# A decoder trunk on one core: the roots of the last row tiles' norms on GpSimd, and sums that keep their place in the program

## The chip, the core and the metric

The kernel runs on one core of a Trainium2 chip. Its time is the device time of one execution in microseconds, the median of several runs. The engines are TensorE (PE; PEld is its weight load), VectorE (DVE), ScalarE (ACT), GpSimd (POOL) and SyncE (SP), which issues the transfers here. Each engine works through its own queue in order, and semaphores tie the queues together.

## What is computed

One layer of a hybrid decoder for a prompt of 2048 rows and a group of 32 sample rows. The change lies in its end: the mixed groups (2048 columns, `mix`) go through the output projection, are normalised, added to the residual, and normalised again:

```python
def rms_norm(x, g):
    xf = x.astype(jnp.float32)
    y = xf * lax.rsqrt(jnp.mean(xf * xf, axis=-1, keepdims=True) + EPS)
    return (y * g.astype(jnp.float32)).astype(x.dtype)
...
    out = rms_norm(mix @ w_out, post_g)
    return x + out, conv_new, pool_new, k, v
...
    y_prompt = rms_norm(xp, final_g)
```

So each row of the output needs two reciprocal roots: one of the mean square of the projection's row, one of the mean square of the row after the residual is added.

## The kernel before

The earlier stages (norm and input projection, sample group, causal attention of the prompt, convolution) are not touched. In the last stage the 2048 rows are 16 row tiles of 128, taken as 8 pairs i = 0 to 7; i = 8 (`LAST`) stands for the sample rows, which are row tile 16 in the closings. The product `mix @ w_out` is done by a scheme of seven products of half sized blocks, numbered 1 to 7, in which sums and differences of blocks save the eighth. A part is (product, pair, half of its depth): 12 matmuls, each factor split into a high and a low piece (`mh`, `ml` for the rows, `wohi`, `wolo` for the weights), and three products of pieces for each of 4 slices: high by high, high weights' low piece, and last the rows' low piece. TensorE takes the parts in the order of the list `order`: products 1, 7, 2, 6, then 4, 5 and 3, pair by pair. For pairs 3 to 7 that is (4,i), (5,i), (3,i), two halves each.

For each part, in the order of the program: `out_load` (SP brings the rows, L1648 on), `out_combine` (L1694: a sum or difference of two blocks, on GpSimd at L1699, L1702 and L1706, on VectorE at L1705), `out_high` (ScalarE casts to the high piece, L1714), `out_low` (VectorE subtracts to get the low piece, L1725), and the matmuls (L1969). For product 5 the combination is the sum of the two blocks that product 4 loaded, in the tile `mr4_i_h`, at L1699. A part is combined four parts ahead of the one that TensorE is given.

When a product is done, `out_ready` (L1731) joins it with the others. For products 4, 5 and 3 VectorE adds the partial sums `U2` or `U3` (L1768, L1769), ScalarE squares the result and sums it by row (`square`, L1727), and VectorE multiplies it in place by the post factor `gpost` (L1772). Product 5 completes row tile 2i + 1, product 3 row tile 2i, and each is then closed by `out_tile` (L1790): a root of the first mean square (add L1798, root L1799, reciprocal L1800), two products with the residual's row `oxt` added (L1804), two squares (L1805), a second root (L1808 to L1810), a product with the final factor (L1815), and the transfer out (L1817). For even tiles the first half of the row comes back from DRAM as `oh`, with the factor put on by GpSimd (L1788). The two roots' values are columns of a small tile, `oss`, of which there is one buffer. For tile 14, the last, the work of tile 15's end is written between its steps, and its output goes in two halves.

The order on an engine is not that of the text: a scheduler moves instructions ahead where it takes their inputs to be there. `tc.keep_in_program_order` pins one behind the instruction that was written before it on the same engine.

Of the kernel before, what the change touches and what calls it, by code (L numbers as in the profile page):

```python
# [8 lines left out]
F32 = mybir.dt.float32  # L9
# [3 lines left out]
AF = mybir.ActivationFunctionType  # L13
ALU = mybir.AluOpType
# [4 lines left out]
P = 128  # L19
D = 1024  # L20
# [28 lines left out]
RAWS = 4  # L49
# [38 lines left out]
def kernel(  # L88
# [72 lines left out]
                       pattern=[[-1, P]], channel_multiplier=1)  # L161
    ones_ln = con.tile([P, P], F32, name="ones_ln")
    pool.memset(ones_ln, 1.0 / 512)
    eps_t = con.tile([P, 1], F32, name="eps_t")
    pool.memset(eps_t, EPS)
    first = zc.tile([P, 1], F32, name="first")

    table = [act.activation(out=first, in_=eps_t, func=AF.Sqrt)]
# [1525 lines left out]
    def out_combine(x):  # L1694
        prod, i, h = x
        store()
        ts = raws[x]
        if prod == 5 and i < LAST:
            pool.tensor_tensor(out=ts[1], in0=ts[0], in1=ts[1], op=ALU.add)  # L1699
            ts = ts[1:]  # L1700
        elif prod == 7:
            pool.tensor_tensor(out=ts[0], in0=ts[0], in1=ts[1], op=ALU.subtract)  # L1702
            stores.append(((0, i, h), msd[0, i, h], ts[0]))
        elif prod == 6:
            tc.keep_in_program_order(dve.tensor_tensor(out=ts[0], in0=ts[0], in1=ts[1], op=ALU.subtract))  # L1705
            pool.tensor_tensor(out=ts[2], in0=ts[2], in1=ts[0], op=ALU.subtract)  # L1706
            stores.append(((1, i, h), msd[1, i, h], ts[2]))
        raws[x] = ts[0]

# [16 lines left out]

    def square(c, t, half):  # L1727
        rows = P if t < 16 else NS
        act.activation(out=junk[:rows], in_=c[:rows], func=AF.Square, accum_out=ssk[:rows, t, half : half + 1])

    def out_ready(prod, i, o):  # L1731

        if i == LAST:
            if prod == 5:
                return
            both = (ope.tile([P, 512], F32, tag="oh", name="both3", bufs=OH) if prod == 3 else
                    op.tile([P, 512], F32, name=f"both{prod}", bufs=1))
            act.copy(both[:NS], o[NS : 2 * NS])
            dve.tensor_tensor(out=both[:NS], in0=both[:NS], in1=o[:NS], op=ALU.add)
            if prod == 1:  # L1740
                keep["s"] = both
# [12 lines left out]
        if prod == 1:  # L1754
            act.copy(U2[:, i], o)
        elif prod == 7:
            dve.tensor_tensor(out=U3[:, i], in0=o, in1=U2[:, i], op=ALU.add)
        elif prod == 6:
            dve.tensor_tensor(out=U3[:, i], in0=o, in1=U3[:, i], op=ALU.add)
            dve.tensor_tensor(out=U2[:, i], in0=o, in1=U2[:, i], op=ALU.add)  # L1760
        elif prod == 2:
            c = opw.tile([P, 512], F32, tag="c11", name=f"c11_{i}", bufs=1)
            dve.tensor_tensor(out=c, in0=o, in1=U2[:, i], op=ALU.add)
            square(c, t, 0)
            sp.dma_start(c11d[i], c)
        else:
            if prod == 5:
                dve.tensor_tensor(out=U2[:, i], in0=o, in1=U2[:, i], op=ALU.add)  # L1768
            dve.tensor_tensor(out=o, in0=o, in1=(U2 if prod == 3 else U3)[:, i], op=ALU.add)  # L1769
            half = 0 if prod == 4 else 1  # L1770
            square(o, t, half)
            dve.tensor_tensor(out=o, in0=o, in1=gpost[:, 512 * half : 512 * half + 512], op=ALU.mult)  # L1772
            keep[t, half] = o
            if prod != 4:
                out_tile(t, keep[t, 0], keep[t, 1])
            if (prod, i) == (3, 0):
                out_first(2)
            if prod == 5 and i != 2 or (prod, i) == (3, 1):
                out_factor(2 if prod == 3 else i)
# [10 lines left out]
    def out_tile(t, a, b):  # L1790

        rows = P if t < 16 else NS
        xt = ope.tile([P, D], F32, tag="oxt", name=f"oxt{t}", bufs=OX)[:rows]
        sp.dma_start(xt, xp[P * t : P * t + P, :] if t < 16 else xs)
        if t != 14:
            keep["ss"] = ope.tile([P, 6], F32, tag="oss", name=f"oss{t}", bufs=1)
        ss = keep["ss"][:rows, 3:] if t == 14 else keep["ss"][:rows]
        dve.tensor_tensor(out=ss[:, 0:1], in0=ssk[:rows, t, 0:1], in1=ssk[:rows, t, 1:2], op=ALU.add)  # L1798
        act.activation(out=ss[:, 0:1], in_=ss[:, 0:1], func=AF.Sqrt, bias=eps_t[:rows], scale=1.0 / D)  # L1799
        dve.reciprocal(out=ss[:, 0:1], in_=ss[:, 0:1])  # L1800
        last = t == 14
        halves = (slice(0, 512), slice(512, 1024))
        for n, (hs, src) in enumerate(zip(halves, (a[:rows], b[:rows]))):
            dve.scalar_tensor_tensor(out=xt[:, hs], in0=src, scalar=ss[:, 0:1], in1=xt[:, hs], op0=ALU.mult, op1=ALU.add)  # L1804
            act.activation(out=junk[:rows], in_=xt[:, hs], func=AF.Square, accum_out=ss[:, n + 1 : n + 2])  # L1805
        if last:
            keep.pop("end")()
        dve.tensor_tensor(out=ss[:, 1:2], in0=ss[:, 1:2], in1=ss[:, 2:3], op=ALU.add)  # L1808
        act.activation(out=ss[:, 1:2], in_=ss[:, 1:2], func=AF.Sqrt, bias=eps_t[:rows], scale=1.0 / D)  # L1809
        dve.reciprocal(out=ss[:, 1:2], in_=ss[:, 1:2])  # L1810
        dst = y_prompt[0, P * t : P * t + P, :] if t < 16 else y_sample.rearrange("b t d -> (b t) d")

        def end():
            for n, hs in enumerate(halves if last else (slice(0, 1024),)):
                dve.scalar_tensor_tensor(out=xt[:, hs], in0=xt[:, hs], scalar=ss[:, 1:2], in1=gfin[:rows, hs],  # L1815
                                         op0=ALU.mult, op1=ALU.mult)
                (wq if n else sp).dma_start(dst[:, hs], xt[:, hs])  # L1817

        if t == 15:
            keep["end"] = end  # L1820
        else:
            end()
# [261 lines left out]
    for n, x in enumerate(parts):  # L2084
        if n == last_:
# [4 lines left out]
            gfin = ope.tile([P, D], F32, name="gfin", bufs=1)  # L2090
            sp.dma_start(gpost, post_g[0].partition_broadcast(P))
            sp.dma_start(gfin, final_g.partition_broadcast(P))
        prod, i, h = x
        if prod == 4 and not h and i != 2:
            out_first(i)
# [53 lines left out]
```

## Time and profile before

| | |
|---|---|
| median of 3 runs | 2359.39 us (2356.07 to 2364.3) |
| the profiled execution's own time | 2357.87 us |
| its span, first to last instruction | 2356.2 us |
| mean granted TensorE clock | 0.992 |
| TensorE, VectorE, ScalarE, GpSimd busy | 2268.6, 1718.0, 1118.3, 1280.6 us |

In the profile a row of a group gives line, engine, operation, output and inputs by tile name, shapes and count, then busy time and mean duration in ns, then the idle time of the engine ahead of it and what ended that. A row of a timeline gives start, duration and the same names, with the idle time before it in brackets. Names come without their numbers there: `acc` is a product's sum, `mr` a part's rows, `oss` the roots' tile.

### The profile page before, as it was taken

The page shows a single profiled execution, that of the slowest core. Times are in us where ns is not written, and L with a number is a line of the kernel's source. Part 1 is how long each engine was busy: PE and PEld are TensorE (multiplying, and loading weights), DVE is VectorE, ACT ScalarE, POOL GpSimd, SP SyncE. Part 2 cuts the span into 40 slices and gives each one's busy share as a digit, 9 for nine tenths or more (in the row PEclk, how much of TensorE's full clock was granted, in tenths as well). Part 3 has the DMA queues.
Part 4 walks back from the last instruction along what each step waited for, and adds up shares of the span by engine and source line. Part 5 has one row for each costly group of instructions (what it writes and reads, how often), then busy time and mean ns, then how long its engine had stood idle before and what let it go on. Part 6 is the DMA issues. An engine that isn't in the chain of part 4 may idle for free. (4 is left out here: it accounts for less than half of the span.)

```text
span 2356.2 us, 42223 instructions
## 1 busy us (share of the span) xinstructions
PE 2268.6 (96%) x16024; PEld 1767.5 (75%) x16024; DVE 1718.0 (73%) x2428; ACT 1118.3 (47%) x1947; POOL 1280.6 (54%) x1322
## 2 busy tenths in 40 slices
PE   7999999999999999999999999899999999999897
PEld 7998888888888777777777777555555557878775
DVE  5342786969647664577787868888897966787897
ACT  5322343342442322234242324788989875454554
POOL 3554545555464656545546463688988854432330
PEclk9999999999999999999999999999999999999999
DMA  6689977878678899987877884756544207866674
GB/s 212 196 283 298 343 267 257 288 248 289 243 262 314 311 352 338 322 287 260 304 264 257 280 273 143 176 170 165 161 131 117 77 23 225 283 223 215 208 247 159
DMA packets 336870, 557.94 MB, mean 237 GB/s; under 512 B 27986, under 2 KB 212434, under 8 KB 320267
## 3 DMA queue, kind: packets, MB, share of 16 engines
q1 hardware_dynamic: 281290, 286.53, 39.4%
q0 software_dynamic: 55376, 268.72, 32.0%
q8 instruction: 126, 2.06, 0.4%
q14 instruction: 78, 0.63, 0.1%
HBM read 465.09 MB, written 90.68 MB: 236 GB/s over the span
## 5 line engine op out<-in xcount | busy, mean ns | idle before, releaser
L966 DVE STREAM_TRANSPOSE T<-kt 128x1024 f32<-128x1024 f32 x256 | 308.6, 1225 | 182.8 <-PE sSA L979 170.0
L933 POOL DMA_INDIRECT vt<-in_cache_v_dram,idv x256 | 252.8, 988 | 255.5 <-PE sO L1018 194.9
L618 DVE SCALAR_TENSOR_TENSOR cacc<-U,par,cacc 128x512 f32<-128x512 f32 x480 | 359.7, 749 | 11.0
L1344 POOL TENSOR_TENSOR be<-be,E 128x512 f32<-128x512 f32 (+3 forms) x316 | 300.6, 967 | 60.4 <-DVE E L1335 26.6
L1335 DVE TENSOR_TENSOR_SCAN E<-gam,cr,ZM 128x513 f32<-128x513 f32 x192 | 232.7, 1262 | 14.1 <-ACT gam L1266 10.7
L933 POOL DMA_INDIRECT kt<-in_cache_k_dram,idk x128 | 128.3, 1002 | 198.8 <-DVE T L966 157.4
L1355 PEld LDWEIGHTS AT<-ident,be 128*128 128x128 f32 x1082 | 116.1, 141 | 128.0 <-ACT at L1361 48.2
L1969 PE MATMUL acc<-wohi,mh 128*128 128x512 f32 (+1 forms) x480 | 193.5, 403 | 1.9 <-ACT mh L1714 1.9
L1266 ACT ACTIVATE gam<-S,nbias_bc 128x1024 f32<-128x1024 f32 (+1 forms) x158 | 173.1, 1095 | 42.6 <-ACT be L1267 18.5
L1969 PE MATMUL acc<-wolo,mh 128*128 128x512 f32 (+1 forms) x480 | 189.5, 395 | 2.6 <-DVE wolo L1626 2.6
L1969 PE MATMUL acc<-wohi,ml 128*128 128x512 f32 x448 | 177.4, 396 | 5.6 <-DVE ml L1725 5.6
L1262 PE MATMUL S<-kT,Q 128*128 128x512 f32 (+1 forms) x632 | 174.6, 399 | 5.4 <-ACT be L1267 5.4
L1267 ACT ACTIVATE be<-S,bias_bc 128x1024 f32<-128x1024 f32 (+1 forms) x158 | 172.0, 1089 | 1.4 <-DMA gsd<-sg1sg 1.4
L1355 PE MATMUL AT<-ident,be 128*128 128x128 f32 x1082 | 157.3, 283 | 14.0 <-DVE at L1359 7.4
L1371 PE MATMUL av<-at,V 128*64 128x512 f32 (+3 forms) x640 | 152.2, 554 | 3.5 <-DVE sbo L1376 3.5
L979 PE MATMUL sSA<-T,W 128*32 128x128 f32 x4096 | 138.3, 276 | 1.8 <-DVE T L966 1.4
L979 PEld LDWEIGHTS sSA<-T,W 128*32 128x32 f32 x4096 | 104.6, 109 | 36.6 <-issue 29.1
L1018 PE MATMUL sO<-vt,saT 128*32 128x512 f32 x1024 | 122.3, 592 | 0.0
L1725 DVE TENSOR_TENSOR ml<-mr,mh 128x512 fp32r<-128x512 f32 x108 | 95.7, 897 | 35.0 <-ACT mh L1714 33.5
L1262 PEld LDWEIGHTS S<-kT,Q 128*128 128x128 f32 x632 | 105.0, 193 | 19.2 <-ACT be L1267 6.8
L1361 ACT COPY at<-AT 128x512 f32<-128x512 f32 x192 | 111.3, 679 | 12.2 <-PE AT L1355 12.2
L1332 DVE TENSOR_TENSOR_SCAN E<-gam,ZM 128x384 f32<-128x384 f32 (+1 forms) x124 | 94.3, 809 | 28.8 <-ACT gam L1266 22.0
(577 smaller groups left out, 6024.7 us busy)
## 6 DMA issues: line engine op xcount, KB each, us to landing
Q<-qd SPq DMA_DIRECT2D x64, 256.0 KB
mr<-mixd SPq DMA_DIRECT2D x32, 512.0 KB
mr<-mixd SPq DMA_DIRECT2D x48, 256.0 KB
xtp<-in_x_prompt_dram SPq DMA_DIRECT2D x16, 512.0 KB
kT<-kd SPq DMA_DIRECT2D x64, 128.0 KB
ws<-in_w_out_dram SPq DMA_DIRECT2D x16, 512.0 KB
wsd<-ws SPq DMA_DIRECT2D x16, 512.0 KB
msd<-mr SPq DMA_DIRECT2D x32, 256.0 KB
```

Of the source, the lines that this page charges most:

```text
L618: dve.scalar_tensor_tensor(out=ps, in0=U[:, a + k : a + k + H], scalar=wd[:, k : k + 1], in1=ps, op0=ALU.mult, op1=ALU.add)
L933: pool.indirect_dma_start(out=dst, out_offset=None, in_=rows, in_offset=bass.IndirectOffsetOnAxis(ap=idx, axis=0))
L966: S["turn"] = dve.transpose(T[:, 2 * hh : 2 * hh + 2].rearrange("p s j t -> p (s j t)"), kt[:, 2 * hh : 2 * hh + 2].rearrange("p s j d -> ...
L979: pe.matmul(sSs[n][32 * g : 32 * g + 32, P * ml : P * (ml + 1)], lhsT=W[:, jj, :], rhs=T[:, :, jj, :], start=i == 0, stop=i == 3, tile_pos ...
L1262: pe.matmul(S[:, j, :w], lhsT=Q[:, x, P * (q2 + j) : P * (q2 + j + 1)], rhs=kt[:, :w], start=x == 0, stop=x == 1)
L1266: act.activation(out=ga, in_=S[:, :, :w], func=AF.Sigmoid, bias=nbias_bc[:, h : h + 1], scale=-1.0)
L1267: act.activation(out=be, in_=S[:, :, :w], func=AF.Sigmoid, bias=bias_bc[:, h : h + 1])
L1335: dve.tensor_tensor_scan(out=E[:, j][:, ::-1], data0=g_[:, j][:, ::-1], data1=ZM[:, 0:1].to_broadcast([P, 513]), initial=carry[hh, q2][:, ...
L1344: newest.append(pool.tensor_tensor(out=be[:, j, :m], in0=be[:, j, :m], in1=E[:, j, 513 - w : 513 - w + m], op=ALU.mult).ins)
L1355: pe.transpose(ap_[:, P * qt : P * (qt + 1)], A[hp, qb, kc, hh, qt][:, P * r : P * (r + 1)], ident)
L1371: pe.matmul(av[64 * hh : 64 * hh + 64, c], lhsT=V[:, 4 * kc + r, 64 * hh : 64 * hh + 64], rhs=ats.pop((hp, qb, kc, r, hh))[:, c], start=dg ...
L1969: pe.matmul(o[:rows], lhsT=m[a][:, k, :rows], rhs=W[prod, 4 * h + k][w], start=not cont and h == k == n == 0, stop=h == 1 and k == 3 and n ...
```

## The change

Four things. The roots of row tiles 10 to 15 are two GpSimd instructions: one adds the two halves' mean squares and epsilon, one raises the sum to the power of -0.5. The other tiles keep their three instructions on VectorE and ScalarE. The mean's factor goes into the squares (`scale=D**-0.5`), so the roots need none. The post factor of products 4 and 5 is put on when product 5 is done, and for pair 7 into a tile of its own (`og`) instead of in place. GpSimd's sum of product 5 and its difference of product 6 are pinned. `oss` becomes one tile with two sets of four columns in turn.

```diff
-    eps_t = con.tile([P, 1], F32, name="eps_t")
+    two = con.tile([P, 2], F32, name="two")
+    eps_t, mhalf = two[:, 0:1], two[:, 1:2]
     pool.memset(eps_t, EPS)
+    pool.memset(mhalf, -0.5)
...
         if prod == 5 and i < LAST:
-            pool.tensor_tensor(out=ts[1], in0=ts[0], in1=ts[1], op=ALU.add)
+            tc.keep_in_program_order(pool.tensor_tensor(out=ts[1], in0=ts[0], in1=ts[1], op=ALU.add))
...
-            pool.tensor_tensor(out=ts[2], in0=ts[2], in1=ts[0], op=ALU.subtract)
+            tc.keep_in_program_order(pool.tensor_tensor(out=ts[2], in0=ts[2], in1=ts[0], op=ALU.subtract))
...
-        act.activation(out=junk[:rows], in_=c[:rows], func=AF.Square, accum_out=ssk[:rows, t, half : half + 1])
+        act.activation(out=junk[:rows], in_=c[:rows], func=AF.Square, scale=D**-0.5, accum_out=ssk[:rows, t, half : half + 1])
...
             square(o, t, half)
-            dve.tensor_tensor(out=o, in0=o, in1=gpost[:, 512 * half : 512 * half + 512], op=ALU.mult)
             keep[t, half] = o
             if prod != 4:
+                for n in (0, 1) if prod == 5 else (1,):
+                    c = keep[t, n]
+                    if i == LAST - 1:
+                        keep[t, n] = op.tile([P, 2, 512], F32, tag="raw", name=f"og{t}_{n}", bufs=RAWS)[:, 0]
+                    dve.tensor_tensor(out=keep[t, n], in0=c, in1=gpost[:, 512 * n : 512 * n + 512], op=ALU.mult)
                 out_tile(t, keep[t, 0], keep[t, 1])
...
-        dve.tensor_tensor(out=ss[:, 0:1], in0=ssk[:rows, t, 0:1], in1=ssk[:rows, t, 1:2], op=ALU.add)
-        act.activation(out=ss[:, 0:1], in_=ss[:, 0:1], func=AF.Sqrt, bias=eps_t[:rows], scale=1.0 / D)
-        dve.reciprocal(out=ss[:, 0:1], in_=ss[:, 0:1])
+        keep["turn"] = 4 - keep.get("turn", 4)
+        ss = oss[:rows, keep["turn"] : keep["turn"] + 4]
+
+        def root(k, a, b):
+            if not 10 <= t < 16:
+                dve.tensor_tensor(out=ss[:, k : k + 1], in0=a, in1=b, op=ALU.add)
+                act.activation(out=ss[:, k : k + 1], in_=ss[:, k : k + 1], func=AF.Sqrt, bias=eps_t[:rows])
+                dve.reciprocal(out=ss[:, k : k + 1], in_=ss[:, k : k + 1])
+                return
+            pool.tensor_scalar(out=ss[:, k : k + 1], in0=b, scalar1=a, scalar2=EPS, op0=ALU.add, op1=ALU.add)
+            pool.tensor_tensor(out=ss[:, k : k + 1], in0=ss[:, k : k + 1], in1=mhalf[:rows], op=ALU.pow)
+
+        root(0, ssk[:rows, t, 0:1], ssk[:rows, t, 1:2])
...
-        dve.tensor_tensor(out=ss[:, 1:2], in0=ss[:, 1:2], in1=ss[:, 2:3], op=ALU.add)
-        act.activation(out=ss[:, 1:2], in_=ss[:, 1:2], func=AF.Sqrt, bias=eps_t[:rows], scale=1.0 / D)
-        dve.reciprocal(out=ss[:, 1:2], in_=ss[:, 1:2])
+        root(3, ss[:, 1:2], ss[:, 2:3])
```

How this moves instructions is seen at three places. The first is GpSimd's queue from the sum for part (5,6,0) on, before the change. Here `mr4_6_1` and `mr4_7_1` are the sums for parts (5,6,1) and (5,7,1), and `oh2_i` the post factor on tile 2i's first half:

```order
L1699 TENSOR_TENSOR mr4_6_0_23612<-mr4_6_0_23612 128x512
L1699 TENSOR_TENSOR mr4_6_1_23633<-mr4_6_1_23633 128x512
L1788 TENSOR_TENSOR oh2_5_23596<-oh2_5_23596,gpost_22691 128x512
L1699 TENSOR_TENSOR mr4_7_0_23764<-mr4_7_0_23764 128x512
L1699 TENSOR_TENSOR mr4_7_1_23785<-mr4_7_1_23785 128x512
L1788 TENSOR_TENSOR oh2_6_23748<-oh2_6_23748,gpost_22691 128x512
L1788 TENSOR_TENSOR oh2_7_23902<-oh2_7_23902,gpost_22691 128x512
```

The same place after the change. The first "..." leaves out the six rows of the other three roots of tiles 11 and 10, the second the eight rows of tiles 13 and 12:

```order
L1701 TENSOR_TENSOR mr4_6_0_23603<-mr4_6_0_23603 128x512
L1794 TENSOR_TENSOR oh2_6_23733<-oh2_6_23733,gpost_22692 128x512
L1701 TENSOR_TENSOR mr4_7_0_23749<-mr4_7_0_23749 128x512
L1810 TENSOR_SCALAR oss_22696<-ssk_20133 128x1
L1811 TENSOR_TENSOR oss_22696<-oss_22696,two_93 128x1
...
L1701 TENSOR_TENSOR mr4_6_1_23623<-mr4_6_1_23623 128x512
L1794 TENSOR_TENSOR oh2_7_23881<-oh2_7_23881,gpost_22692 128x512
...
L1701 TENSOR_TENSOR mr4_7_1_23769<-mr4_7_1_23769 128x512
```

The sums for (5,6,1) and (5,7,1) have moved behind all four roots of the two tiles closed before them; the four roots of tiles 15 and 14 follow the last row.

The second place is VectorE's queue around the low piece of part (5,6,1), `ml5_6_1`. Before the change it stands inside tile 11's closing:

```order
L1804 SCALAR_TENSOR_TENSOR oxt11_23672<-acc4_5_23598,oss11_23674,oxt11_23672 128x512
L1804 SCALAR_TENSOR_TENSOR oxt11_23672<-acc5_5_23638,oss11_23674,oxt11_23672 128x512
L1769 TENSOR_TENSOR acc3_5_23691<-acc3_5_23691,U2_20130 128x512
L1725 TENSOR_TENSOR ml5_6_1_23767<-mr4_6_1_23633,mh5_6_1_23766 128x512
L1808 TENSOR_TENSOR oss11_23674<-oss11_23674 128x1
L1772 TENSOR_TENSOR acc3_5_23691<-acc3_5_23691,gpost_22691 128x512
```

After the change:

```order
L1826 SCALAR_TENSOR_TENSOR oxt11_23663<-oxt11_23663,oss_22696,gfin_22693 128x1024
L1771 TENSOR_TENSOR acc3_5_23679<-acc3_5_23679,U2_20131 128x512
L1780 TENSOR_TENSOR acc3_5_23679<-acc3_5_23679,gpost_22692 128x512
L1817 SCALAR_TENSOR_TENSOR oxt10_23715<-oh2_5_23587,oss_22696,oxt10_23715 128x512
L1817 SCALAR_TENSOR_TENSOR oxt10_23715<-acc3_5_23679,oss_22696,oxt10_23715 128x512
L1771 TENSOR_TENSOR acc4_6_23735<-acc4_6_23735,U3_20132 128x512
L1826 SCALAR_TENSOR_TENSOR oxt10_23715<-oxt10_23715,oss_22696,gfin_22693 128x1024
L1727 TENSOR_TENSOR ml5_6_1_23752<-mr4_6_1_23623,mh5_6_1_23751 128x512
L1727 TENSOR_TENSOR ml3_6_0_23772<-mr3_6_0_23693,mh3_6_0_23771 128x512
```

The low piece has moved behind the whole closings of tiles 11 and 10.

The third place is the end of VectorE's queue, tile 15's first part after the change (before it, the rows are those of the profile, with the factor in place and the add and the reciprocal between):

```order
L1770 TENSOR_TENSOR U2_20131<-acc5_7_23918,U2_20131 128x512
L1771 TENSOR_TENSOR acc5_7_23918<-acc5_7_23918,U3_20132 128x512
L1780 TENSOR_TENSOR og15_1_23953<-acc5_7_23918,gpost_22692 128x512
L1817 SCALAR_TENSOR_TENSOR oxt15_23955<-og15_0_23951,oss_22696,oxt15_23955 128x512
L1817 SCALAR_TENSOR_TENSOR oxt15_23955<-og15_1_23953,oss_22696,oxt15_23955 128x512
L1826 SCALAR_TENSOR_TENSOR oxt15_23955<-oxt15_23955,oss_22696,gfin_22693 128x1024
L1771 TENSOR_TENSOR acc3_7_23966<-acc3_7_23966,U2_20131 128x512
```

Tile 15's last product now comes ahead of the first add of tile 14, and nothing of one column is left between them.

More of the change, by code (lines that the diff above doesn't have):

```diff
@@ L1794, in out_tile @@
         sp.dma_start(xt, xp[P * t : P * t + P, :] if t < 16 else xs)
[L1795 to L1800, printed above, removed]
+        keep["turn"] = 4 - keep.get("turn", 4)
[9 more added lines that the diff above has]
+        root(0, ssk[:rows, t, 0:1], ssk[:rows, t, 1:2])
         last = t == 14
@@ L1804, in out_tile @@
             dve.scalar_tensor_tensor(out=xt[:, hs], in0=src, scalar=ss[:, 0:1], in1=xt[:, hs], op0=ALU.mult, op1=ALU.add)
-            act.activation(out=junk[:rows], in_=xt[:, hs], func=AF.Square, accum_out=ss[:, n + 1 : n + 2])
+            act.activation(out=junk[:rows], in_=xt[:, hs], func=AF.Square, scale=D**-0.5, accum_out=ss[:, n + 1 : n + 2])
         if last:
             keep.pop("end")()
-        dve.tensor_tensor(out=ss[:, 1:2], in0=ss[:, 1:2], in1=ss[:, 2:3], op=ALU.add)
-        act.activation(out=ss[:, 1:2], in_=ss[:, 1:2], func=AF.Sqrt, bias=eps_t[:rows], scale=1.0 / D)
-        dve.reciprocal(out=ss[:, 1:2], in_=ss[:, 1:2])
+        root(3, ss[:, 1:2], ss[:, 2:3])
         dst = y_prompt[0, P * t : P * t + P, :] if t < 16 else y_sample.rearrange("b t d -> (b t) d")
@@ L1814, in end @@
             for n, hs in enumerate(halves if last else (slice(0, 1024),)):
-                dve.scalar_tensor_tensor(out=xt[:, hs], in0=xt[:, hs], scalar=ss[:, 1:2], in1=gfin[:rows, hs],
+                dve.scalar_tensor_tensor(out=xt[:, hs], in0=xt[:, hs], scalar=ss[:, 3:4], in1=gfin[:rows, hs],
                                          op0=ALU.mult, op1=ALU.mult)
@@ L2092 @@
             sp.dma_start(gfin, final_g.partition_broadcast(P))
+            oss = ope.tile([P, 8], F32, name="oss", bufs=1)
         prod, i, h = x
```

## The prediction

> **What bounds the kernel now.** I read the page first, for its engines and its chain that ended last.
>
> ```profile
> span 2356.2 us, 42223 instructions
> PE 2268.6 (96%) x16024; PEld 1767.5 (75%) x16024; DVE 1718.0 (73%) x2428; ACT 1118.3 (47%) x1947; POOL 1280.6 (54%) x1322
> ```
>
> TensorE is busy 96% of the span, so almost every microsecond that the change can win or lose is one in which TensorE does not multiply. There are two kinds of those: holes between matmuls, and the stretch after the last one. The windows of the last stage and the waits of the output matmuls between 2200 and 2340 us show both.
>
> ```profile
> 2260.00:2300.00 40.00, 40.00 (x176) 32.80 (x175) 37.94 (x68) 22.01 (x60) 13.75 (x10) 1.00 0.72 242
> 2300.00:2320.00 20.00, 20.00 (x88) 16.32 (x88) 18.70 (x33) 9.60 (x27) 2.18 (x2) 1.00 0.61 208
> PE acc L1969 <- DVE ml L1725: 3.8, 2, 3.5
> PE acc L1969 <- DVE wolo L1626: 2.6, 1, 2.6
> ```
>
> After the span and the length, the columns are TensorE, weight load, VectorE, ScalarE and GpSimd. From 2260 us on TensorE has no hole, with VectorE busy 37.94 of 40 us: VectorE nearly fills the time too, and what TensorE needs is ready only because it was made early. A matmul takes 20/88 = 0.227 us, a part (12 of them) 2.73 us, and a row tile's closing begins every two parts or four. The holes before that (3.5 and 2.6 us) are at weights and low parts. The rest is the tail, in the order of time on TensorE, VectorE and ScalarE:
>
> ```profile
> 2339.09 0.40 PE L1969 MATMUL acc<-wohi,ml 128*128 128x512 f32 x1
> 2339.33 0.68 DVE L1768 TENSOR_TENSOR U<-acc,U 128x512 f32<-128x512 f32 x1
> 2339.93 0.69 DVE L1769 TENSOR_TENSOR acc<-acc,U 128x512 f32<-128x512 f32 x1
> 2341.43 0.70 DVE L1772 TENSOR_TENSOR acc<-acc,gpost 128x512 f32<-128x512 f32 x1 [0.81 <-ACT junk L1729]
> 2342.04 0.15 DVE L1798 TENSOR_TENSOR oss<-ssk 128x1 f32<-128x1 f32 x1
> 2342.74 1.41 DVE L1804 SCALAR_TENSOR_TENSOR oxt<-acc,oss,oxt 128x512 f32<-128x512 f32 x2
> 2344.07 0.69 DVE L1769 TENSOR_TENSOR acc<-acc,U 128x512 f32<-128x512 f32 x1
> 2345.09 0.16 DVE L1808 TENSOR_TENSOR oss<-oss 128x1 f32<-128x1 f32 x1 [0.33 <-ACT junk L1805]
> 2346.60 1.28 DVE L1815 SCALAR_TENSOR_TENSOR oxt<-oxt,oss,gfin 128x1024 f32<-128x1024 f32 x1
> 2348.05 0.75 DVE L1804 SCALAR_TENSOR_TENSOR oxt<-oh,oss,oxt 128x512 f32<-128x512 f32 x1
> 2350.40 0.16 DVE L1808 TENSOR_TENSOR oss<-oss 128x1 f32<-128x1 f32 x1 [0.93 <-ACT junk L1805]
> 2351.12 1.41 DVE L1815 SCALAR_TENSOR_TENSOR oxt<-oxt,oss,gfin 128x512 f32<-128x512 f32 x2
> ```
>
> TensorE ends at 2339.49, the span at 2356.2: a tail of 16.7 us. VectorE starts tile 15's closing (2339.33) only when TensorE is already through with tile 14, although product 5 of tile 15 was finished two parts (5.5 us) earlier: tile 12's closing stood before it. So the tail holds two closings in a row, and the last 3.7 us (2352.53 to 2356.2) are the output's transfer.
>
> **What the change takes away.** For tiles 10 to 15 it removes two adds, two reciprocals and two square roots each.
>
> ```profile
> L1800 DVE RECIPROCAL oss<-oss 128x1 f32<-128x1 f32 x16 | 2.5, 155 | 1.8 <-ACT oss L1799 1.7
> L1798 DVE TENSOR_TENSOR oss<-ssk 128x1 f32<-128x1 f32 x16 | 2.3, 146 | 0.0
> L1799 ACT ACTIVATE oss<-oss,eps_t 128x1 f32<-128x1 f32 x16 | 4.7, 294 | 21.9 <-DVE oss L1798 21.8
> ```
>
> That is 12 x (0.146 + 0.155) = 3.6 us of VectorE and 12 x 0.294 = 3.5 us of ScalarE. In the tail one root costs what lies from its add to its user, 2342.04 to 2342.74 and 2350.40 to 2351.12: **0.70 us**. The factor apart from the square also takes L1772 (0.61 to its successor) out of the way between square and root. The scale within the squares changes no duration.
>
> **What a root costs on GpSimd (r).** No row shows a power, nor a 128x1 operation but a fill. The nearest:
>
> ```profile
> L170 POOL MEMSET zeros<- 128x1 f32 x1 | 0.1, 100 | 0.0
> L1340 POOL COPY cr<-E 128x2 f32<-128x2 f32 x96 | 18.3, 191 | 8.8 <-DVE E L1335 5.0 <-DVE E L1332 2.3
> L739 POOL TENSOR_TENSOR us_s<-us_s,sg0cb 128x32 f32<-128x32 f32 x4 | 1.0, 254 | 0.0
> 2299.59 1.29 POOL L1699 TENSOR_TENSOR mr<-mr 128x512 f32<-128x512 f32 x1 [2.29 <-ACT mh L1714]
> ```
>
> Two fills and three handings-over of 0.03 (2342.19 to the root's start at 2342.22 in the old chain is one) are 0.3; a copy and a power as long as a whole 128x512 sum, 0.19 + 1.29 + 0.1, are 1.6. I take **r = 0.7**: the copy (0.19) for the sum, some 0.4 for the power (a short two-input operation, 0.25, and half as much again, an estimate), 0.1 for handing over. So a root is not faster than before; it only leaves VectorE and ScalarE.
>
> **What the change moves.** Product 4's factor now waits for product 5; the work is the same, and only VectorE's own queue hides it. If that cover is gone it is worth a hole like those above, 0 to 2.6 us, most likely nothing. The sums of product 5 matter more. In the old order GpSimd did the sum for part (5,6,1) long before its use:
>
> ```profile
> 2283.27 1.29 POOL L1699 TENSOR_TENSOR mr<-mr 128x512 f32<-128x512 f32 x1 [2.14 <-DMA mr<-mixd]
> 2304.68 0.68 DVE L1768 TENSOR_TENSOR U<-acc,U 128x512 f32<-128x512 f32 x1
> 2330.08 0.61 ACT L1714 CAST mh<-mr 128x512 fp32r<-128x512 f32 x1
> 2330.82 0.68 DVE L1725 TENSOR_TENSOR ml<-mr,mh 128x512 fp32r<-128x512 f32 x1
> ```
>
> The first row is that sum (seventh from the end in GpSimd's order). TensorE wants the part at 2339.09 + 0.23 - 9 x 2.73 = 2314.8 us, so there were 30 us to spare. Now the sum stands on GpSimd behind both roots of tiles 11 and 10, each of which waits for its squares, and behind it wait ScalarE's cast, VectorE's low part and TensorE.
>
> VectorE begins tile 11 at 2304.7 (the second row, tile 11's add into U2). By the tail's rows: two adds 1.29, square 0.81, root r, two products 1.41, second squares 0.94 (2344.15 to 2345.09), root r, last product 1.28; then tile 10: add 0.69, 0.81, r, 1.41, 0.94, r. In all 9.6 + 4r, 12.4 at r = 0.7, so the sum starts at 2317.1. Sum 1.29, cast 0.65 and low part 0.68: 2319.7, and 2320.4 if tile 10's last product (1.28 on VectorE) has to wait for the sum. That it does is likely:
>
> ```profile
> 2185.65 5.03 POOL L1699 TENSOR_TENSOR mr<-mr 128x512 f32<-128x512 f32 x1 [2.81 <-DMA mr<-mixd]
> 2299.69 2.28 DVE L1815 SCALAR_TENSOR_TENSOR oxt<-oxt,oss,gfin 128x1024 f32<-128x1024 f32 x1
> ```
>
> The last product takes 2.28 instead of 1.28 us beside the sum at 2299.59, and another sum took 5.03 instead of 1.29. [...] The third matmul of the part, the first on a low part, is due at 2315.3: TensorE waits 4.4 to 5.1 us, I take **4.7**.
>
> For part (5,7,1), behind tiles 13 and 12, the same happens a period of 16.4 us later, but the first hole lets VectorE catch up: free after four more products of 0.6 at 2322.8, sum at 2335.2, low part 2337.8 to 2338.4, wanted at 2336.4: **1.7**. TensorE ends 6.4 us later.
>
> The tail then: VectorE has no arrears when product 5 of tile 15 ends, so both closings follow from there: 1.29 + 0.81 + r + 1.41 + 0.94 + r + 1.28, then 0.69 + 0.81 + r + 1.41 + 0.94 + r + 1.41, and 3.67 for the transfer: 14.66 + 4r = 17.5, less the two parts that TensorE still multiplies beside it (5.46): **12.0 in place of 16.7**, 4.7 won.
>
> Sum: + 6.4 - 4.7 = + 1.7 us on the profiled execution's 2357.87, which is 1.5 under the median of the three runs; on the median it is **2361 us**.
>
> **The rivals.**
> 1. *GpSimd's power is long (slower).* r counts four times before each held sum and four times in the tail: 12 us per us of r. From r = 1.15 the sum is over + 7.1 us; at r = 1.6 it is 8.3 + 5.3 - 1.1 = + 12.5, 2372 us. [...] Against it: copies of a few columns take 0.19.
> 2. *The held sums arrive in time (faster).* TensorE ends product 5 of tile 11 fourteen parts before 2339.49, at 2301.3, and VectorE turns to it only at 2304.7. Without the small work and its waits it may do so up to 3.4 us sooner, and a root of 0.3 in place of 0.7 gives 1.6 more: together over 4.7. No hole: - 4.7, 2354.7; with r = 0.3 the tail is 10.4, - 6.3, 2353. Also the hole of 3.5 us could close in the moved order of the sums, which would carry it over - 7.1. Against it: VectorE's 18.70 of 20 us leaves little to catch up with.
> [...]
>
> **How the numbers follow.** Forecast 0.50; long power 0.28; sums in time 0.17; code 0.05. A measurement tells 0.3%, 7.1 us, from no change. Faster than that is half of the second rival: 0.09. Slower is the first rival with some of the forecast's upper end: 0.31. The rest is 0.60. The range reaches from the second rival at a short root (2353) to the first at its bound (2372).
>
> **What would show it.** In the profile after: rows of 128x1 on GpSimd, a pair from square to user in 0.7 us; a wait of TensorE of 4 to 5 us at its output matmuls for the low part near 2315, and one under 2 near 2336; holes nowhere else from 2260 on; a tail of 12 us. The forecast is wrong if the power's row is over 0.8 us, if those waits are missing, or if VectorE is still in arrears at tile 15.

## The result, and the profile after

The changed kernel takes 2371.33 us in the median of 7 runs (2368.94 to 2373.26), the kernel before 2362.48 beside it: a ratio of **1.0038, 95% interval 1.0024 to 1.0051**. In a second series (run 11 below) it is 1.0043, 1.0027 to 1.0058. So it is slower by some 9 us, 0.38%. That is more than the 0.3% that a measurement tells from no change, though the interval begins below it. The forecast was 2361 and "no change"; the range to 2372 just holds the time.

The profiled execution has a span of 2371.6 us, 15.4 over the one before. The two executions stand differently to their medians: that of before took 2357.87, 4.6 under the median of its 7 runs, that of after 2373.26, 1.9 over its own. So 6.5 of the 15.4 us are put down to the choice of the execution, and 8.9 are to be explained.

In the changed file the matmul is L1980 (L1969 before), product 5's sum L1701 (L1699), the high piece L1716, the low piece L1727, the adds into the partial sums L1770 and L1771, the post factor L1780 and, on GpSimd, L1794, the closing's products L1817 and L1826, the second squares L1818; GpSimd's root is L1810 (add) and L1811 (power). These are the waits of TensorE at its output matmuls from 2260 us on, in the timeline of the kernel after; before, there was none:

```profile
2280.54 0.50 PE L1980 MATMUL acc<-wohi,ml 128*128 128x512 f32 x1 [1.24 <-DVE ml L1727]
2324.81 0.80 PE L1980 MATMUL acc<-wohi,mh 128*128 128x512 f32 x1 [5.98 <-ACT mh L1716]
2326.93 0.80 PE L1980 MATMUL acc<-wohi,ml 128*128 128x512 f32 x1 [0.90 <-DVE ml L1727]
2346.57 0.50 PE L1980 MATMUL acc<-wohi,mh 128*128 128x512 f32 x1 [1.80 <-ACT mh L1716]
2347.61 0.79 PE L1980 MATMUL acc<-wohi,ml 128*128 128x512 f32 x1 [0.31 <-DVE ml L1727]
```

The two that were forecast are there, at parts (5,6,1) and (5,7,1): 6.88 and 2.11 us (two waits each) where 4.7 and 1.7 were expected. They were looked for at the low parts; most of each (5.98 and 1.80 us) stands at the high piece ahead of it, whose cast the late sum holds as well. GpSimd's timeline shows what they wait for: the sum starts when the fourth root in front of it is through.

```profile
2311.80 0.58 POOL L1811 TENSOR_TENSOR oss<-oss,two 128x1 f32<-128x1 f32 x1
2321.95 0.29 POOL L1810 TENSOR_SCALAR oss<-oss 128x1 f32<-128x1 f32 x1 [2.44 <-ACT junk L1818]
2322.32 0.55 POOL L1811 TENSOR_TENSOR oss<-oss,two 128x1 f32<-128x1 f32 x1
2322.85 1.25 POOL L1701 TENSOR_TENSOR mr<-mr 128x512 f32<-128x512 f32 x1
2344.61 1.25 POOL L1701 TENSOR_TENSOR mr<-mr 128x512 f32<-128x512 f32 x1
```

The same windows hold something that no step of the prediction had. The last column but two is the clock that TensorE was granted:

```profile
2312.00:2318.00 6.00, 6.00 (x29) 4.95 (x28) 3.94 (x6) 1.67 (x5) 1.23 (x3) 1.00 0.28 93
2325.00:2328.00 3.00, 2.10 (x5) 1.19 (x6) 3.00 (x5) 1.88 (x5) 1.32 (x1) 0.50 0.44 178
2328.00:2332.00 4.00, 4.00 (x15) 3.16 (x14) 2.24 (x5) 0.62 (x1) 0.00 (x0) 0.73 0.56 179
2347.00:2350.00 3.00, 2.69 (x8) 1.91 (x7) 2.45 (x4) 1.13 (x4) 0.00 (x0) 0.54 0.43 175
```

Behind each of these two holes TensorE runs at half its clock for a while: matmuls start every 0.43 us instead of 0.23, until about 2330.1 and 2350.6. Eleven steps between matmuls are that long in this trace, 2.2 us lost, and some 0.7 more at the restarts.

The tail, from TensorE's end (2357.18) to the span's end, is 14.4 us. VectorE's rows in it, with GpSimd's last root and the closing drain of its queue (range of durations in ns, first and last start):

```profile
2351.61 0.69 DVE L1770 TENSOR_TENSOR U<-acc,U 128x512 f32<-128x512 f32 x1 [2.07 <-PE acc L1980]
2358.13 1.28 DVE L1826 SCALAR_TENSOR_TENSOR oxt<-oxt,oss,gfin 128x1024 f32<-128x1024 f32 x1 [1.96 <-POOL oss L1811]
2364.66 0.55 POOL L1811 TENSOR_TENSOR oss<-oss,two 128x1 f32<-128x1 f32 x1
2365.24 1.41 DVE L1826 SCALAR_TENSOR_TENSOR oxt<-oxt,oss,gfin 128x512 f32<-128x512 f32 x2 [1.96 <-POOL oss L1811]
```
```profile
L2157 POOLq DRAIN  x3: 40/102/6160, 2364.6 to 2371.3; - x3
```

VectorE is idle when product 5 of tile 15 is done (2.07 us waiting for TensorE), as forecast. But the two closings take 15.04 us (2351.61 to 2366.65) where they took 13.20 before (2339.33 to 2352.53), and from the last product to the end it is 4.95 instead of 3.67 us.

### The profile page after: what moved, and what is told of

Same layout as the page of the kernel before. It is cut to its first block, busy times and chain, and to the rows that moved or that the text cites. A ratio compares the mean times of both kernels' runs of the same rounds, so it can differ in the third digit from the quotient of the medians.

```text
span 2371.6 us, 42225 instructions
## 1 busy us (share of the span) xinstructions
PE 2272.9 (96%) x16024; PEld 1769.3 (75%) x16024; DVE 1713.3 (72%) x2404; ACT 1115.0 (47%) x1935; POOL 1292.2 (54%) x1347
## 5 line engine op out<-in xcount | busy, mean ns | idle before, releaser
L1980 PE MATMUL acc<-wohi,mh 128*128 128x512 f32 (+1 forms) x480 | 194.2, 405 | 9.5 <-ACT mh L1716 9.5
L1980 PE MATMUL acc<-wolo,mh 128*128 128x512 f32 (+1 forms) x480 | 190.1, 396 | 0.7 <-DVE wolo L1628 0.7
L1980 PE MATMUL acc<-wohi,ml 128*128 128x512 f32 x448 | 178.3, 398 | 6.8 <-DVE ml L1727 6.8
L1727 DVE TENSOR_TENSOR ml<-mr,mh 128x512 fp32r<-128x512 f32 x108 | 93.1, 874 | 33.1 <-ACT mh L1716 32.9
```

Source lines behind the costliest of these rows:

```text
L1980: pe.matmul(o[:rows], lhsT=m[a][:, k, :rows], rhs=W[prod, 4 * h + k][w], start=not cont and h == k == n == 0, stop=h == 1 and k == 3 and n ...
```

## The experiments

Theory 1, the prediction's own: product 5's sums, pinned behind the roots, make the holes, so that without the pin the change would be a gain. Theory 2: the roots on GpSimd cost the time by themselves, because VectorE waits for them in its order. Theory 3: the pins or the moved factor cost it without any root on GpSimd. "Holes" are the sums of TensorE's waits from about 2260 us on (half clock is noted for these alone), and "tail" is TensorE's end to the span's end, all of the one profiled execution of each run; the ratio is of all runs to the kernel before in the same series.

| run | roots on GpSimd | pins (sum of 5, difference of 6) | ratio (95%) | holes | half clock behind them | tail |
|---|---|---|---|---|---|---|
| before | none | none | 1 | 0 | no | 16.7 |
| after | 10 to 15 | both | 1.0038 (1.0024 to 1.0051) | 10.2 | yes | 14.4 |
| 1 | 10 to 15 | 6 | 1.0024 (1.0011 to 1.0038) | 3.4 | no | 17.8 |
| 2 | 14, 15 | both | 0.9997 (0.9983 to 1.0011) | 1.5 | no | 17.4 |
| 3 | none | both | 0.9987 (0.9975 to 0.9999) | 1.4 | no | 14.3 |
| 4 | none, old factor | both | 1.0012 (1.0001 to 1.0024) | 2.7 | no | 17.2 |
| 5 | none, a fill | both | a single execution, 2356.22 us | 1.9 | no | 14.2 |
| 6 | 10 to 13 | both | 1.0023 (1.0009 to 1.0038) | 10.8 | yes | 12.0 |
| 7 | none | none | 0.9989 (0.9974 to 1.0004) | 0.2 | no | 15.8 |
| 8 | none | 6 | 0.9992 (0.9977 to 1.0006) | 1.7 | no | 15.9 |
| 9 | 10 to 15 | both, idle work | 1.0036 (1.0022 to 1.0049) | 4.0 + 7.6 of idle work | no | 14.4 |
| 10 | 10 to 13 | 6 | 1.0006 (0.9991 to 1.0020) | 3.3 | no | 14.9 |
| 11 | 10 to 15 | both | 1.0043 (1.0027 to 1.0058) | 10.4 | yes | 14.4 |

### Run 1: product 5's sum free

```diff
-            tc.keep_in_program_order(pool.tensor_tensor(out=ts[1], in0=ts[0], in1=ts[1], op=ALU.add))
+            pool.tensor_tensor(out=ts[1], in0=ts[0], in1=ts[1], op=ALU.add)
```

> The changed kernel, with only the pin on product 5's sum (L1701) taken away: the two sums for parts (5,6,1) and (5,7,1) are again early in GpSimd's queue, ahead of all twelve roots. Theory 1 (the sums pinned behind the roots make the holes, and the low clock after each hole comes with it): the waits of 5.98 + 0.90 us near 2325 and of 1.80 + 0.31 us near 2347 go, and the granted clock in those places stays at 1.00 instead of 0.50 and 0.54; what is left of the change is its tail, 14.4 instead of 16.7 us, so about 2.3 us under before, a ratio of 0.998 to 1.000. Theory 2 (the roots on GpSimd cost the time by themselves, since VectorE waits for them in order, 0.97 us and the handing over instead of 0.70, and the low parts stand behind the closings in VectorE's queue): a wait of 2 to 5 us at the low parts of (5,6,1) or (5,7,1) stays with the sum done long before, ratio 1.002 to 1.004. Theory 3 (the other pin, the moved factor or the squares' scale cost it): as the changed kernel, 1.004.

Measured: 2364.63 us, 1.0024 (1.0011 to 1.0038). The big holes are gone, and the clock stays at 1.00. But theory 1's number (0.998 to 1.000) is missed, and the reason is theory 2's. TensorE still waits at the low parts of (5,6,1) and its neighbours:

```profile
2310.05 0.50 PE L1980 MATMUL acc<-wohi,ml 128*128 128x512 f32 x1 [0.31 <-DVE ml L1727]
2313.91 0.50 PE L1980 MATMUL acc<-wohi,ml 128*128 128x512 f32 x1 [0.84 <-DVE ml L1727]
2317.18 0.50 PE L1980 MATMUL acc<-wohi,ml 128*128 128x512 f32 x1 [0.23 <-DVE ml L1727]
2321.51 0.50 PE L1980 MATMUL acc<-wohi,ml 128*128 128x512 f32 x1 [1.27 <-DVE ml L1727]
```

VectorE's timeline of this run shows why, for the second and the last of them:

```profile
2311.37 1.29 DVE L1826 SCALAR_TENSOR_TENSOR oxt<-oxt,oss,gfin 128x1024 f32<-128x1024 f32 x1 [1.37 <-POOL oss L1811]
2312.57 0.69 DVE L1771 TENSOR_TENSOR acc<-acc,U 128x512 f32<-128x512 f32 x1
2313.17 0.68 DVE L1727 TENSOR_TENSOR ml<-mr,mh 128x512 fp32r<-128x512 f32 x1
...
2318.48 1.29 DVE L1826 SCALAR_TENSOR_TENSOR oxt<-oxt,oss,gfin 128x1024 f32<-128x1024 f32 x1 [0.75 <-POOL oss L1811]
2319.69 1.77 DVE L1727 TENSOR_TENSOR ml<-mr,mh 128x512 fp32r<-128x512 f32 x1
```

The low part that TensorE wants stands behind a last product that waits 1.37 us for its root; the part is ready at 2313.85, and the matmul starts at 2313.91. The last wait has a second share: the low part takes 1.77 instead of 0.68 us, beside GpSimd's post factor (2318.61, 2.29 us long). And without the long hole nothing gives VectorE time to catch up: it turns to tile 15 at 2338.61, 3.3 us after product 5 was through (the two last parts, 5.46 us, end at 2340.74), and the tail is 17.8 instead of 14.4 us. Holes and tail together are 21.1 us, 4.4 over the kernel before; the changed kernel has 24.6, and the half clock.

### Runs 2 and 3: fewer roots on GpSimd, or none

```diff
-            if not 10 <= t < 16:
+            if not 14 <= t < 16:
```
```diff
-            if not 10 <= t < 16:
+            if not 99 <= t < 16:
```

> The changed kernel with the roots on GpSimd for row tiles 14 and 15 alone; 10 to 13 keep add, square root and reciprocal on VectorE and ScalarE. Both pins stay. Theory 1: with no root of tiles 10 to 13 on GpSimd nothing is in front of the pinned sums, no hole at (5,6,1) and (5,7,1), the tail as in the changed kernel (14.4 us): ratio 0.998 to 1.000, like the first run. Theory 2: tiles 10 to 13 cost nothing more, so no hole either, 0.998 to 1.000, and the first run stays 2 to 5 us above this one. Theory 3: pins and factor are still there, 1.004.

> The changed kernel with no root on GpSimd at all: all tiles keep add, square root and reciprocal; both pins, the factor behind product 5 and the scale in the squares stay. Theories 1 and 2: no holes at (5,6,1) and (5,7,1); the tail is that of before (16.7 us) or shorter by what the moved factor gives (0 to 1.2 us): ratio 0.9995 to 1.0005, and so 1 to 2 us above the second run. Theory 3: 1.004.

Measured: 0.9997 (0.9983 to 1.0011) and 0.9987 (0.9975 to 0.9999). Theory 3 is out: both pins with the moved factor do not make the changed kernel slow. Theories 1 and 2 were both wrong in the tail, where they had run 2 ahead: with two tiles' roots on GpSimd it is 17.4, with none 14.3 us, so run 3 and not run 2 is ahead (2.4 us by the ratios, 3.2 by the profiles; the intervals overlap). The start of tile 15 and the last product, run 2 and then run 3:

```profile
2338.09 0.68 DVE L1770 TENSOR_TENSOR U<-acc,U 128x512 f32<-128x512 f32 x1
2351.76 1.41 DVE L1826 SCALAR_TENSOR_TENSOR oxt<-oxt,oss,gfin 128x512 f32<-128x512 f32 x2 [1.96 <-POOL oss L1811]
```
```profile
2342.65 0.68 DVE L1770 TENSOR_TENSOR U<-acc,U 128x512 f32<-128x512 f32 x1
2354.44 1.42 DVE L1826 SCALAR_TENSOR_TENSOR oxt<-oxt,oss,gfin 128x512 f32<-128x512 f32 x2
```

The last pair of closings takes 15.08 us with GpSimd's roots and 13.21 without, and the span ends 4.93 and 3.64 us after it: 3.2 us in all. In run 3 VectorE puts tile 14's first add into the wait for tile 15's second squares; in run 2 that add stands behind tile 15's last product, and VectorE waits 1.96 us. How much of the 1.87 us between the closings is the length of the roots and how much is this order was not told apart.

### Run 4: the kernel before with the two pins

The two `tc.keep_in_program_order` alone, nothing else of the change.

> The kernel before with the two pins alone (the sum of product 5 and the difference of product 6 keep their source place on GpSimd); roots and factor as before. Theories 1 and 2: GpSimd's sums stand where their loads are, no root in front, ratio 0.9995 to 1.0005. Theory 3, if the pins are what costs: the moved sums open holes earlier (those of 2.60 and 3.51 us of before grow or new ones come), 1.002 to 1.004.

Measured: 1.0012 (1.0001 to 1.0024), just above what theories 1 and 2 allowed and under theory 3's 1.002. Its profile has waits of 1.21, 0.29, 0.34 and 0.88 us for low parts from 2280 to 2333, where the kernel before has none. The holes near 2200 and 2236 did not grow (4.6 us with the one near 2230, against 6.4). So the pins alone cost a little with the old factor, and in run 3, with the moved factor, nothing that can be measured.

### Run 5: one fill on GpSimd in the tail

Run 3's kernel, and in it:

```diff
         root(3, ss[:, 1:2], ss[:, 2:3])
+        if t == 14:
+            pool.memset(ss[:, 1:2], 0.0)
```

> The third run's kernel (no root on GpSimd) with one fill of 128x1 on GpSimd in the tail: it sets a column of the sums to zero that nobody reads any more, after tile 14's second add. In the changed kernel GpSimd's closing drain took 6.16 us from before the end of the last power (0.55 of it beside that power) and ended at 2370.8, about 1.3 us after what the output's transfer needs; in the third run the same drain took 7.16 us from 2325.3 on and was over by 2332.5, far from the end. Theory D (whatever GpSimd does last, its drain ends 5.6 us later, and this sets the end of the kernel): the fill alone brings it back, 4.9 us instead of 3.6 from the last product to the end, with everything ahead of it unchanged. Rival (the power itself needs the long drain, or the transfer is slower for another reason): 3.6 us as in the third run.

The fill, the last product and GpSimd's closing drain:

```profile
2348.07 0.10 POOL L1823 MEMSET oss<- 128x1 f32 x1 [24.81 <-DVE oss L1806]
...
2348.57 1.41 DVE L1828 SCALAR_TENSOR_TENSOR oxt<-oxt,oss,gfin 128x512 f32<-128x512 f32 x2
```
```profile
L2159 POOLq DRAIN  x3: 40/102/5687, 2348.0 to 2354.3; - x3
```

A fill of 0.10 us, for which nobody waits, moves the end of the span: 4.5 us after the last product (2349.98 to 2354.5) instead of 3.64. The drain ends at 2353.7, 5.55 us after the fill; in the changed kernel it ends at 2370.8, 5.55 us after the last power; in run 3, below, 5.55 us after GpSimd's last factor (2325.34 and 1.57 long), with 27 us to spare.

```profile
L2157 POOLq DRAIN  x3: 40/102/7163, 2325.3 to 2359.2; - x3
```

Some 0.8 us behind the drain the span ends, in both kernels. It is 4.5 and not the expected 4.9 because the fill ends 0.40 us before the last product starts, the last power only 0.03. Theory D holds in this one execution: the power is not needed for it. The tail as a whole, 14.2 us, is no longer than in run 3, because VectorE turned to tile 15 earlier here, 3.56 us ahead of TensorE's end (2336.77, 2340.33) and not 2.58 (2342.65, 2345.23).

### Run 6: roots of tiles 10 to 13 alone

```diff
-            if not 10 <= t < 16:
+            if not 10 <= t < 14:
```

> The changed kernel with the roots on GpSimd for row tiles 10 to 13 alone; 14 and 15 keep add, square root and reciprocal. Both pins stay, so both product 5 sums stand behind four roots each, as in the changed kernel. Theory 1 (behind the pinned sums TensorE waits and then runs at half clock): the same holes of 6 to 7 us and of 2 us, each followed by a stretch of 3.4 us or more at a clock of 0.50; the tail is shorter than the changed kernel's 14.4 by the longer roots and the drain, 1.85 + 1.3, so 11.3 us: the time 3 us under the changed kernel, ratio 1.0025 against before. Theory 2 (the roots cost it wherever they are): as much is lost in the two middle pairs as in the last, and the ratio is 1.0010 to 1.0020 with smaller holes.

Measured: 1.0023 (1.0009 to 1.0038), 2368.68 us. Holes and clock come as theory 1 has them:

```profile
2319.87 0.79 PE L1980 MATMUL acc<-wohi,mh 128*128 128x512 f32 x1 [6.01 <-ACT mh L1716]
2322.00 0.79 PE L1980 MATMUL acc<-wohi,ml 128*128 128x512 f32 x1 [0.91 <-DVE ml L1727]
2342.21 0.50 PE L1980 MATMUL acc<-wohi,mh 128*128 128x512 f32 x1 [1.79 <-ACT mh L1716]
```
```profile
2320.00:2324.00 4.00, 3.09 (x7) 1.99 (x8) 4.00 (x6) 1.95 (x5) 1.39 (x1) 0.50 0.47 148
```

The tail is 12.0 us (11.3 expected): closings of 13.79 and 3.78 us to the end. It is the number that was forecast for the changed kernel, and it needs the old roots. Against the changed kernel the gain is not shown, as the intervals overlap (1.0023 and 1.0038); in the profiled execution the half clock lasts longer, 17 steps of 0.43 us behind the two holes in place of 11.

### Runs 7 and 8: what of the change is left without roots on GpSimd

Run 7 is run 3 without both pins, run 8 run 3 without the pin of product 5's sum.

> The changed kernel with no root on GpSimd and neither pin: what is left of the change is the factor behind product 5 and the scale in the squares. If the factor is what made the third run's tail 14.3 instead of 16.7 us (the small VectorE work ahead of the last pair is done earlier), it is here too, with no small holes of 1.2 to 1.4 us near 2280 but with the 2.6 and 3.5 us holes near 2200 and 2236 of the kernel before: ratio 0.9985 to 1.0000. If the pins made it, the tail is 16.7 us and the ratio 1.000.

> As the run before it, but with product 6's differences pinned (product 5's sums are free). If the pin of product 6 is what shortens the holes near 2200 and 2236 (from 6.4 to 3.1 to 4.6 us in all in the runs with it) and the pin of product 5 opens the one near 2280 (0.7 us in the first run, without it, against 1.2 to 1.5), this is the fastest of all: ratio 0.998 to 0.999. If not, it is like the third run, 0.9987.

Measured: 0.9989 (0.9974 to 1.0004) and 0.9992 (0.9977 to 1.0006); tails of 15.8 and 15.9 us, holes of 0.2 and 1.7 us from 2260 on. The tail of run 7 is nearly a microsecond under 16.7 with no pin at all, as expected of the factor; with both pins it is 14.3 and 14.2 (runs 3 and 5), with the pins and the old factor 17.2 (run 4), which speaks for both being needed; these are single executions, and the closings themselves take 13.2 us in before, run 3 and run 7 alike, so the difference lies in when VectorE gets to tile 15. Run 8 was expected to lack the wait near 2280 us if product 5's pin opened it; with that pin gone the wait is 1.73 us, so that pin is not needed for it. The order of runs 3, 7 and 8 is not told by intervals this wide. Run 3 is 0.13% under the kernel before, with an interval that ends just under 1 and is the only one here to do so; among ten intervals that can be chance, and a gain is not shown.

### Runs 9 and 11: TensorE kept at work through the holes

```diff
         o, m = accs[bank], mix.pop(x)
+        w = W[prod, 4 * h][0]
+        for _ in range({(5, 6, 1): 25, (5, 7, 1): 7}.get(x, 0)):
+            pe.matmul(o, lhsT=w[:, :P], rhs=w, start=False, stop=False)
```

> The changed kernel with idle work for TensorE ahead of the two held parts: 25 matmuls of 128x512 ahead of part (5,6,1) and 7 ahead of (5,7,1), both operands weights that have lain in SBUF long since (row tiles 12 to 15 so get a product that does not belong to them; nothing else differs). At 0.23 us each they last 5.75 and 1.6 us, just under the holes of 5.98 and 1.80 us, so they delay nothing. Theory C (a hole of TensorE costs a second time, by the half clock after it, and that clock follows from TensorE's idleness): the parts behind the holes start when they did and run a matmul in 0.23 instead of 0.43 us; TensorE ends 3.3 us earlier (2.0 + 1.3) and the kernel is 3.3 us under the changed kernel of this call, ratio about 1.0024 against before. Rival (the matmuls behind the holes are slow because their low parts or weights come late): they keep 0.43 us each, time as the changed kernel.

> The changed kernel itself once more, beside the two runs before it, so that a difference of 3 us can be read within one series. All theories: ratio 1.003 to 1.004, holes of 6.0 + 0.9 and 1.8 + 0.3 us at the same parts, a clock of 0.50 behind each, 4.9 us from the last product to the end.

Measured: 2369.56 us, 1.0036 (1.0022 to 1.0049), against 2373.48 us, 1.0043 (1.0027 to 1.0058), for the changed kernel in the same series. The medians are 3.9 us apart, near the 3.3 that theory C gave, but the intervals overlap, so the proof is in the profile. The idle work takes 5.83 and 1.75 us, and the clock does not fall behind it; first run 9, then run 11:

```profile
2325.00:2328.00 3.00, 1.91 (x8) 1.61 (x9) 3.00 (x5) 1.05 (x3) 0.48 (x1) 1.00 0.59 196
2328.00:2332.00 4.00, 4.00 (x19) 3.19 (x19) 3.18 (x6) 1.93 (x4) 0.86 (x2) 1.00 0.78 248
2347.00:2350.00 3.00, 3.00 (x14) 2.43 (x13) 1.54 (x3) 0.69 (x2) 0.00 (x0) 1.00 0.00 0
```
```profile
2328.00:2332.00 4.00, 3.10 (x7) 1.99 (x8) 4.00 (x6) 2.00 (x5) 1.44 (x1) 0.50 0.47 150
2351.00:2354.00 3.00, 2.88 (x7) 2.30 (x8) 1.96 (x4) 0.64 (x2) 0.00 (x0) 0.53 0.43 175
```

From the first matmul of part (5,6,1) to TensorE's end it is 29.5 us in run 9 (2323.97 to 2353.47) and 32.9 in run 11 (2327.92 to 2360.86). The same low parts, weights and neighbours, only TensorE was at work before them: in these two places the half clock follows from its idleness, and it costs 3.4 us on top of 9 us of holes. (Run 9 has a stretch of half clock too, but elsewhere: from 2232.70 to 2236.22, behind a wait of 2.60 us that had no idle work in it.)

### Run 10: roots of tiles 10 to 13, product 5's sum free

Run 6 with the edit of run 1.

> As the sixth run (roots on GpSimd for tiles 10 to 13 alone), with product 5's sum free again, ahead of the roots. Theory 1 (the pin is what costs in the middle pairs): the holes of 6.0, 0.9, 1.8 and 0.3 us and both stretches at half clock go, and the ratio falls from the sixth run's 1.0023 to the third's 0.999. Theory 2 (the roots on GpSimd delay VectorE, which then makes the low parts of these and of the next parts late, and has arrears at the last pair): small holes of 0.2 to 1.3 us at low parts remain, as in the first run (2.65 us in four), and TensorE's end to the span's end is longer than the third run's 14.3; ratio 1.000 to 1.002.

Measured: 1.0006 (0.9991 to 1.0020), between the two theories' numbers. The four small waits of run 1 are here again in the same sizes (0.29, 0.84, 0.22 and 1.27 us), with two more of 0.38 and 0.31; the tail is 14.9 us, the clock stays at 1.00 from 2260 us on. From run 6 the pin is worth 0.0017 (4 us), from the changed kernel to run 1 0.0014 (3.3 us), each with an uncertainty of about its own size. In the profiles, holes and tail together fall by 4.6 (22.8 to 18.2) and 3.5 us (24.6 to 21.1), and the half clock of 3 us goes in both. Run 1 against run 8, which differs from it in the roots alone, is what roots on GpSimd cost with no sum pinned behind them: 0.0032 (7.6 us), and the intervals stand apart.

## Why it came out otherwise, step by step

**The bound held.** What the change costs is found in TensorE's holes, its clock and the tail. From the matmul ahead of the first wait near 2200 us, which in both kernels has the same 594 matmuls behind it, to the end of the span it is 160.5 us before (from 2195.72) and 170.3 after (from 2201.26). That is 9.9 us more, beside 8.9 between the medians; the other 5.5 of the 15.4 us lie ahead of that place. The parts: from 2260 us on the changed kernel has 10.2 us of holes, some 3.4 of half clock (runs 9 and 11) and a tail shorter by 2.3, 11.3 more. Between 2190 and 2260 it has 2.9 less (waits of 1.05, 1.75 and 0.67 us for 3.51, 0.24 and 2.60), which leaves 8.4. The rest is in how a wait is read: the idle time in brackets is short of the loss, since the rows of two matmuls overlap (0.39 us long, with a start every 0.23). At 2280.54 the bracket has 1.24 us, while the starts around it come 1.51 us late; five times that difference is 1.4 us, an estimate.

**The root was mis-sized: r = 0.7 was 1.0.** The power's row is short, but there is a gap within the pair and a handing over on each side of it:

```profile
L1811 POOL TENSOR_TENSOR oss<-oss,two 128x1 f32<-128x1 f32 x12 | 6.7, 557 | 1.0
L1810 POOL TENSOR_SCALAR oss<-ssk 128x1 f32<-128x1 f32 x6 | 1.8, 297 | 24.2 <-ACT junk L1731 24.2
L1810 POOL TENSOR_SCALAR oss<-oss 128x1 f32<-128x1 f32 x6 | 1.8, 294 | 14.7 <-ACT junk L1818 14.7
```

The add takes 0.30 where 0.19 was taken from a copy, the power 0.56 for 0.4, the gaps 0.2 for 0.1. In the last closing it is 0.96 us from the add (2364.28) to the product (2365.24), as the forecast counted it, and 1.06 from the squares' end. The forecast named a power's row over 0.8 us as what would prove it wrong; the row was well under that, and the root was too long all the same.

**The first hole, 4.7 forecast, 6.9 measured, is that term with its price corrected.** 9.6 + 4r at r = 1.0 is 13.6; VectorE begins tile 11 at 2309.24, and the sum starts 13.61 later. So the chain was right as a sum, the last product's longer time beside the sum (2.28 us here too, 1.28 for tile 11's without one) and the 0.90 at the low part included. 1.2 of the 2.2 us are r; the rest is that VectorE came to tile 11 half a microsecond later, as TensorE goes, and the steps behind the sum. The second hole, 1.7 forecast, is 2.1.

**The half clock was missing from the sum.** No term had it; it is 3.4 us by runs 9 and 11.

**The tail, 12.0 forecast, 14.4 measured.** Its closings were sized with r, four times 0.3: 15.04 us in place of 13.79, 1.25 more. The other 1.3 is GpSimd's drain, which no step had: the prediction took the output's transfer (3.67) as given, though the change put GpSimd's last instruction next to the end. "VectorE has no arrears at tile 15" held, but for a reason that the prediction had half seen: it is the hole that lets VectorE catch up, and without it (run 1) the arrears are 3.3 us.

**The factor at nothing held.** It is no loss: run 7 is 0.9989, not told from 1. The scale in the squares changed no duration either: a square of a product's sum takes 0.597 us before and after, a second square 0.631 in both (medians). "Holes nowhere else" failed with the 1.24 us at 2280.54. That wait is in all runs with product 6 pinned, 0.4 to 1.9 us, and 0.2 in run 7 without a pin; why it varies so much is open.

**The rivals.** The long power was the right direction under a wrong condition: it asked for r = 1.15, and 1.0 was enough since 4.7 us stood beside it that were in no rival, the half clock and the drain. That the range held the time is luck: its upper end, 2372, is the price of a root of 1.6 us, with a power as long as a whole sum (1.29), and the power took 0.56. The sums in time did not come. The 0.05 that the forecast gives to "code" was the author's guess of a first power some 5 us longer than the others; no run shows such a term: the first power takes 0.58 us (2311.80), the mean of all twelve is 0.557.

**The picture behind the sum** was that holes are the price and the tail the gain, so that, as theory 1 had it, the roots on GpSimd would win without the pin. Runs 1, 2 and 3 took that down. By the medians GpSimd's roots lose in every place where they were tried. The intervals stand apart for tiles 10 to 15 (the changed kernel against run 3, run 1 against run 8) and for tiles 10 to 13 behind the pin (run 6 against run 3); they overlap for tiles 14 and 15 alone (run 2 against run 3) and for tiles 10 to 13 without the pin (run 10 against run 8). The shorter tail that the changed kernel does have is paid for by its holes.

## What to carry to other kernels

An operation that leaves a full engine is not gained if that engine then waits for it in its own order: price the way from the last input to the user, hand-overs included, and look at what stands behind the waiting instruction. When an engine is brought into the tail, ask when it has to be through, not only how long its instructions take (GpSimd's drain ended 5.55 us after its last instruction here). A hole on TensorE is to be counted with the stretch of half clock that can follow it (here 9 us of holes and 3.4 us of half clock, runs 9 and 11).

## What the runs showed of the hardware

- **A hole can cost twice.** Behind waits of 5.98 to 6.02 us (after, runs 6 and 11) and of 1.79 to 1.81 us (with one of 0.3 us soon after) the granted clock falls to 0.50, and matmuls start every 0.43 instead of 0.23 us; with idle matmuls in the hole it stays at 1.00 (run 9). Not each hole does it: that of 3.51 us in the kernel before, which ends at 2199.63, has 1.00 in the window behind it, and that of 3.48 us in run 7 has a stretch of half clock (2206.3 to 2209.7):

```profile
2198.00:2202.00 4.00, 2.37 (x10) 1.99 (x11) 3.72 (x5) 1.80 (x4) 1.62 (x1) 1.00 0.94 314
```
```profile
2204.82 0.50 PE L1980 MATMUL acc<-wohi,ml 128*128 128x512 f32 x1 [3.48 <-DVE ml L1727]
2206.00:2210.00 4.00, 4.00 (x13) 3.10 (x12) 4.00 (x8) 2.23 (x5) 0.11 (x1) 0.57 1.04 414
```

  The length of the wait alone does not decide it. Near 2200 us a wait of 2.22 us is followed by half clock in run 6 (0.50 from 2197 to 2200), and one of 2.20 us in run 1 is not (1.00 from 2196 to 2204). Between 2190 and 2260 us, ahead of the place that the table counts from, the profiles of runs 3 and 5 to 10 have one such stretch of 3.0 to 3.5 us each, behind waits of 1.85 to 3.48 us; the two kernels, runs 1, 2, 4 and 11 have none there, with waits of up to 3.51 us. What besides the length decides is open.
- **GpSimd's closing drain** ends 5.55 us after its last instruction, be that a power, a fill of 0.10 us or a product of 128x512 (after, runs 5 and 3). In after and run 5, where that falls at the end, the span ends 0.8 us behind it; in run 3 the drain has 27 us to spare.
- **GpSimd beside VectorE** costs VectorE in more places than the last product, which took 2.28 us beside GpSimd's sum (after, 2322.91) and 1.28 without one (2315.79): the low part of run 1 took 1.77 instead of 0.68 us beside a GpSimd factor.
